# Attention in a diffusion-transformer block: where the softmax's division is applied, on one Trainium2 core

## The chip, the core and the metric

The kernel runs on one core of a Trainium2 chip. The metric is device time in microseconds (us), from launch to end on the core. TensorE (PE in the profile) does the matmuls, with its weight loads in a row of their own (PEld); VectorE (DVE), ScalarE (ACT) and GpSimd (POOL) do elementwise work; SyncE (SP) issues the transfers. TensorE's clock has two levels, 1.2 and 2.4 GHz, and the profile gives the granted clock as a share of the higher one.

## What is computed

One block of a transformer: a feed-forward part, a mixer, a second feed-forward part. The mixer adds a gated scan and a window attention with a sink. What the change touches is the attention: 512 tokens in four blocks of 128, eight heads of width 64 on two key/value heads, each query block against its own key block and the two beside it, and against 256 context keys.

```python
def softmax_with_sink(logits, sink):
    sink_col = jnp.broadcast_to(sink, logits.shape[:-1] + (1,))
    p = jax.nn.softmax(jnp.concatenate([logits, sink_col], axis=-1), axis=-1)
    return p[..., :-1]
...
    p = softmax_with_sink(jnp.concatenate([s_band, s_ctx], axis=-1), sink_b).astype(v.dtype)
    o = (jnp.einsum('bkgnqs,bknsd->bkgnqd', p[..., :3 * BLOCK], vb)
         + jnp.einsum('bkgnqs,bksd->bkgnqd', p[..., 3 * BLOCK:], vc))
```

All tensors are fp32. The kernel multiplies them in a rounded fp32 form (`F32R`) and keeps precision by splitting an operand into a rounded high part and a remainder, each with a matmul of its own.

## The kernel before, in words

`split(hi, lo, src)` (L64 to L66) makes the two parts: a copy with a cast on ACT (L65), a subtraction on DVE (L66). `mm3` (L68 to L74) multiplies split operands in three matmuls: L71, L72 and L74. Nearly all matmuls of the projections stand on these lines.

The instructions are written in program order, but the framework's scheduler puts each engine's instructions in an order of its own, and each engine runs its own list strictly in that order. So an edit in one place can move instructions of other steps on all engines.

The attention works head by head. Head `(g, kv)` is number `kv * 4 + g`; the loop of L1131 to L1141 runs the scores of a head before the output of the head before it.

- `head_scores` (from L1059) makes, for each of the four query blocks `b`, the scores of the band (`sw`) and of the context (`sc`) with four matmuls (L1073, L1075) into two PSUM tiles of the tag `mm`; DVE adds the mask and finds the negated maximum (L1078, L1080); ACT takes the exponential and the sum of it (L1082) into the tile `s`, the probabilities of the block, 512 or 640 columns wide. When all four sums are there, the sink's exponential is added and the reciprocal taken: L1086 on ACT, L1087 and L1088 on DVE, all on 128x4 elements. Then each of the four tiles is scaled by its reciprocal, the first on ACT (L1092), the three others on DVE (L1094).
- `head_out` (from L1097) transposes the probabilities block by block on PE (L1107, with `ident`), splits them (`pth`, `ptl`) and multiplies them with the values: L1113 with the high part, L1114 with the remainder, into one PSUM tile `oo` of the tag `aux`. The value operand holds its own high and low half side by side, so that the two halves of `oo` are added at the end: an ACT copy (L1117) and a DVE sum (L1118) into `ov`, 64x512, which is split into `oah` and `oal`, the input of the merge.

PSUM tiles have two tags, `mm` and `aux`, of four buffers each. `oo` and the transposes take `aux`.

As work to set between the heads' steps, PE has the gate projections (`early_gate`, five of them, 24 matmuls each on L71, L72, L74) and the query projections (`q_pair`, L1041). After the attention come the remaining gates and eight merges (`merge`, L1150), which multiply `oah`/`oal` and the scan's output `rTh`/`rTl` with their output weights.

Beside the merges runs a background task (`mod_gate`, `mod_cols`, in twelve parts by `mod_part`, L635): each part loads eight pieces of `w_ada` into `b7l` (L640), accumulates them on DVE into `b7h` (L643, L645), splits the sum into `mx` and adds over partitions with two matmuls (L654, L655). `b7h` and `b7l` lie in memory that the attention's pool (`ma`) used, so that the first of these loads waits until the attention lets go of it. Nine of the parts run beside the merges, the other matmuls of L654 and L655 later.

```python
            nc.vector.reciprocal(es, es)
            for b in range(NX):
                nw = (min(b + 2, NX) - max(b - 1, 0)) * P
                if b == 0:
                    nc.scalar.activation(probs[b][:, :nw + L], probs[b][:, :nw + L], AF.Copy, scale=es[:, b:b + 1])
                else:
                    nc.vector.tensor_scalar(probs[b][:, :nw + L], probs[b][:, :nw + L], es[:, b:b + 1], None, ALU.mult)
```

Of the kernel before, what the change touches and what calls it, by code (L numbers as in the profile page):

```python
# [16 lines left out]
P = 128  # L17
# [26 lines left out]
def kernel(ctx: ExitStack, tc: tile.TileContext, i, out):  # L44
# [940 lines left out]
    with tc.tile_pool(name="ma", bufs=1, reuse_waits="tile") as ma:  # L985
# [73 lines left out]
        def head_scores(g, kv, qq):  # L1059
# [26 lines left out]
            nc.scalar.activation(es, nms[:, :, 1], AF.Exp, bias=sk[:, h:h + 1])  # L1086
            nc.vector.tensor_tensor(out=es, in0=es, in1=sums, op=ALU.add)  # L1087
            nc.vector.reciprocal(es, es)  # L1088
            for b in range(NX):
                nw = (min(b + 2, NX) - max(b - 1, 0)) * P  # L1090
                if b == 0:
                    nc.scalar.activation(probs[b][:, :nw + L], probs[b][:, :nw + L], AF.Copy, scale=es[:, b:b + 1])  # L1092
                else:
                    nc.vector.tensor_scalar(probs[b][:, :nw + L], probs[b][:, :nw + L], es[:, b:b + 1], None, ALU.mult)  # L1094
            return probs

        def head_out(g, kv, probs):  # L1097
            rr = slice(64 * kv, 64 * kv + 64)
            oo = ps("aux")
            kts = (4, 0, 1, 2, 3, 5)  # L1100
            for u, kt in enumerate(kts):
                bs = range(NX) if kt >= NX else range(max(kt - 1, 0), min(kt + 2, NX))
                pt = ps("aux")
                for b in bs:
                    w0, w1 = max(b - 1, 0), min(b + 2, NX)
                    off = (kt - w0) * P if kt < NX else (w1 - w0 + kt - NX) * P
                    nc.tensor.transpose(pt[:, b * P:(b + 1) * P], probs[b][:, off:off + P], ident)  # L1107
                cc = slice(bs[0] * P, (bs[-1] + 1) * P)
                th = ct([P, T], "pth", F32R, bufs=3, pool=ma)
                tl = ct([P, T], "ptl", F32R, bufs=3, pool=ma)  # L1110
                split(th[:, cc], tl[:, cc], pt[:, cc])
                vk = vs[:, kt, kv].rearrange("p a b -> p (a b)")
                nc.tensor.matmul(oo[:, cc], lhsT=vk, rhs=th[:, cc], start=u == 0, stop=False)  # L1113
                nc.tensor.matmul(oo[:, cc], lhsT=vk, rhs=tl[:, cc], start=False, stop=u == len(kts) - 1)  # L1114

            ov = ct([P, T], "ov", pool=ma)
            nc.scalar.copy(ov[H[0], :], oo[H[1], :])  # L1117
            nc.vector.tensor_tensor(out=ov[rr, :], in0=oo[H[0], :], in1=ov[H[0], :], op=ALU.add)  # L1118
            split(oah[rr, g, :], oal[rr, g, :], ov[rr, :])

        raw_q = []

        def load_q(u):
# [200 lines left out]
```

## Time and profile before

| | us |
|---|---|
| median of 3 runs | 1462.34 (1461.89 to 1462.94) |
| the profiled execution, its own time | 1462.16 |
| its span, first to last instruction | 1460.4 |
| TensorE busy in the span | 1394.3 (95%) |
| VectorE busy | 1144.2 (78%) |
| ScalarE busy | 663.8 (45%) |
| TensorE's mean granted clock | 0.987 |

The sums in the prediction are made against the profiled execution. The attention's score matmuls start at 811.2 us of the span, the last head's sum (L1118) starts at 929.1 us. A matmul's busy time includes its modelled drain, so that neighbours overlap in the record: what a matmul adds in a row of them is read from start to start.

### The profile page before, as it was taken

The numbers are of one execution on the slowest core, as the hardware profiler recorded it, in microseconds if no ns is written. First come the engines' busy times: TensorE is split into PE (matmuls) and PEld (weight loads), VectorE is DVE, ScalarE is ACT, GpSimd is POOL, SyncE is SP. The second block draws the span as 40 slices with busy tenths as digits, with TensorE's granted clock in tenths as the row PEclk, the third lists the DMA queues.
The fourth block names the chain that finished last, engine by engine and source line by source line (L and its number), as shares of the span: only waits on it lengthen the run. The fifth ranks groups of instructions, "written<-read, shape, count | busy, mean of one in ns | idle before, by whom it ended". The sixth has DMA issues, their size and how long they took to land. (4 is left out here: it accounts for less than half of the span.)

```text
span 1460.4 us, 22968 instructions
## 1 busy us (share of the span) xinstructions
PE 1394.3 (95%) x8864; PEld 1233.6 (84%) x8864; DVE 1144.2 (78%) x1995; ACT 663.8 (45%) x1089; POOL 57.6 (4%) x87
## 2 busy tenths in 40 slices
PE   6899999999999998999999899989898999999997
PEld 3699899999999997889898678767677998999996
DVE  6996888888888777485785789777758987787785
ACT  6544333433333346432335689522247543444442
POOL 3200000000000002000001000000010000000001
PEclk9999999999999999999999899999999999999999
DMA  8343343332333232221212111376534543343211
GB/s 299 115 124 97 98 117 99 102 101 87 101 102 93 73 122 68 83 70 34 71 37 85 35 56 30 111 211 197 174 95 140 167 141 101 103 124 101 87 44 58
DMA packets 195765, 151.61 MB, mean 104 GB/s; under 512 B 8392, under 2 KB 186056, under 8 KB 195656
## 3 DMA queue, kind: packets, MB, share of 16 engines
q1 hardware_dynamic: 195656, 150.15, 34.1%
q8 instruction: 69, 1.13, 0.3%
q14 instruction: 40, 0.33, 0.1%
HBM read 148.02 MB, written 2.10 MB: 103 GB/s over the span
## 5 line engine op out<-in xcount | busy, mean ns | idle before, releaser
L66 DVE TENSOR_TENSOR wl<-wraw,wh 128x1024 fp32r<-128x1024 f32 (+1 forms) x180 | 216.8, 1210 | 78.3 <-ACT wh L65 77.1
L65 ACT CAST wh<-wraw 128x1024 fp32r<-128x1024 f32 (+1 forms) x180 | 184.9, 1031 | 143.7 <-PE aux L429 44.0
L71 PE MATMUL mm<-hh,wh 128*128 128x512 f32 (+2 forms) x488 | 172.6, 357 | 0.3 <-ACT gg L972 0.2
L72 PE MATMUL mm<-hl,wh 128*128 128x512 f32 (+2 forms) x488 | 168.7, 354 | 0.4 <-DVE hl L560 0.3
L74 PE MATMUL mm<-hh,wl 128*128 128x512 f32 (+2 forms) x488 | 160.1, 358 | 4.0 <-DVE wl L66 4.0
L428 PE MATMUL mm<-hh,wh 128*128 128x256 f32 (+1 forms) x400 | 122.3, 306 | 3.9 <-DVE sg L506 3.9
L428 PE MATMUL aux<-hh,wh 128*128 128x256 f32 (+1 forms) x400 | 121.8, 304 | 2.0 <-ACT wh L65 2.0
L430 PE MATMUL aux<-hh,wl 128*128 128x256 f32 (+1 forms) x400 | 121.6, 304 | 0.0
L429 PE MATMUL aux<-hl,wh 128*128 128x256 f32 (+1 forms) x400 | 121.5, 304 | 0.0
L430 PE MATMUL mm<-hh,wl 128*128 128x256 f32 (+1 forms) x400 | 121.4, 303 | 0.0
L429 PE MATMUL mm<-hl,wh 128*128 128x256 f32 (+1 forms) x400 | 121.3, 303 | 0.0
L71 PEld LDWEIGHTS mm<-hh,wh 128*128 128x128 f32 x488 | 92.9, 191 | 14.4 <-ACT gg L972 0.7
L72 PEld LDWEIGHTS mm<-hl,wh 128*128 128x128 f32 x488 | 93.2, 191 | 11.4 <-DVE hl L560 1.6
L74 PEld LDWEIGHTS mm<-hh,wl 128*128 128x128 f32 x488 | 88.6, 191 | 12.3 <-DVE wl L66 5.0
L645 DVE SCALAR_TENSOR_TENSOR macc<-wa,cs,macc 128x256 f32<-128x256 f32 x196 | 88.2, 480 | 13.3 <-DMA wa<-w_ada 12.5
L71 PE MATMUL mm<-woh,act 128*128 128x512 f32 x240 | 94.1, 392 | 0.0
L72 PE MATMUL mm<-wol,act 128*128 128x512 f32 x240 | 93.9, 391 | 0.0
L337 DVE TENSOR_TENSOR tok<-tok,mm 128x512 f32<-128x512 f32 x120 | 76.9, 682 | 12.7 <-PE mm L74 12.5
L428 PEld LDWEIGHTS mm<-hh,wh 128*128 128x128 f32 x400 | 75.9, 190 | 6.5 <-DVE sg L506 5.8
L428 PEld LDWEIGHTS aux<-hh,wh 128*128 128x128 f32 x400 | 75.9, 190 | 2.5 <-ACT wh L65 2.5
L429 PEld LDWEIGHTS mm<-hl,wh 128*128 128x128 f32 x400 | 76.0, 190 | 0.6
L430 PEld LDWEIGHTS mm<-hh,wl 128*128 128x128 f32 x400 | 76.0, 190 | 0.0
(389 smaller groups left out, 3451.5 us busy)
## 6 DMA issues: line engine op xcount, KB each, us to landing
wraw<-ffn_w_in SPq DMA_DIRECT2D x88, 512.0 KB, 4.0
wraw<-mix_w_in SPq DMA_DIRECT2D x42, 512.0 KB, 3.7
wa<-w_ada SPq DMA_DIRECT2D x128, 128.0 KB, 2.1
b7l<-w_ada SPq DMA_DIRECT2D x96, 128.0 KB, 2.7
wraw<-ffn_w_out SPq DMA_DIRECT2D x22, 512.0 KB, 3.3
w<-ffn_w_out SPq DMA_DIRECT2D x22, 512.0 KB, 4.5
wa<-w_ada SPq DMA_DIRECT2D x16, 256.0 KB, 4.2
tok<-w_ada SPq DMA_DIRECT2D x16, 256.0 KB, 5.6
```

The source lines that it names most:

```text
L65: nc.scalar.copy(hi, src)
L66: nc.vector.tensor_tensor(out=lo, in0=src, in1=f32(hi), op=ALU.subtract)
L71: nc.tensor.matmul(o, lhsT=sh, rhs=mh, start=start, stop=False)
L72: nc.tensor.matmul(o, lhsT=sh, rhs=ml, start=False, stop=False)
L74: nc.tensor.matmul(o, lhsT=sl, rhs=mh, start=False, stop=stop)
L337: nc.vector.tensor_tensor(out=y, in0=y, in1=o[h], op=ALU.add)
L428: nc.tensor.matmul(o, lhsT=wk, rhs=mh, start=first and k == 0, stop=False, skip_group_check=True)
L429: nc.tensor.matmul(o, lhsT=wk, rhs=ml, start=False, stop=False, skip_group_check=True)
L430: nc.tensor.matmul(o, lhsT=wl[:, k0 + k, :], rhs=mh, start=False, stop=k == H4 - 1, skip_group_check=True)
L645: nc.vector.scalar_tensor_tensor(out=a, in0=w, scalar=cs[:, v, k:k + 1], in1=a, op0=ALU.mult, op1=ALU.add)
```

## The change

The probabilities stay unscaled. The reciprocals, 128 queries by four blocks, are split into a high part and a remainder (`eh`). In `head_out` eight matmuls per head, two for each query block, spread them over partitions: the stationary operand is one column of `eh` repeated 128 times, the moving operand is the identity in the rounded form (`identr`, made once), so that the PSUM tile `pe` holds, in each of its rows, the reciprocal of query `t` in column `t`. Once the head's output `ov` is summed, one more DVE operation multiplies it with `pe`. In the changed program the lines from L1089 on have other numbers: the transposes are L1104, the value matmuls L1110 and L1111, the spreading matmuls L1117, the sum L1121, the new product L1122.

```diff
             nc.vector.reciprocal(es, es)
-            for b in range(NX):
-                nw = (min(b + 2, NX) - max(b - 1, 0)) * P
-                if b == 0:
-                    nc.scalar.activation(probs[b][:, :nw + L], probs[b][:, :nw + L], AF.Copy, scale=es[:, b:b + 1])
-                else:
-                    nc.vector.tensor_scalar(probs[b][:, :nw + L], probs[b][:, :nw + L], es[:, b:b + 1], None, ALU.mult)
-            return probs
-
-        def head_out(g, kv, probs):
+            eh = [ct([P, NX], f"eh{n}", F32R, bufs=2, pool=ma) for n in range(2)]
+            split(eh[0], eh[1], es)
+            return probs, eh
+
+        def head_out(g, kv, probs_eh):
+            probs, eh = probs_eh
...
+            pe = ps("aux")
+            for b in range(NX):
+                for n in range(2):
+                    nc.tensor.matmul(pe[:, b * P:(b + 1) * P], lhsT=view(eh[n], b, [(0, P)]), rhs=identr,
+                                     start=n == 0, stop=n == 1)
             ov = ct([P, T], "ov", pool=ma)
             nc.scalar.copy(ov[H[0], :], oo[H[1], :])
             nc.vector.tensor_tensor(out=ov[rr, :], in0=oo[H[0], :], in1=ov[H[0], :], op=ALU.add)
+            nc.vector.tensor_tensor(out=ov[rr, :], in0=ov[rr, :], in1=pe[rr, :], op=ALU.mult)
             split(oah[rr, g, :], oal[rr, g, :], ov[rr, :])
 
+        identr = ct([P, P], "identr", F32R, pool=ma)
+        nc.scalar.copy(identr, ident)
```

The scheduler's order moves with it. In these lists a row is line, operation, output, inputs (for a matmul the moving operand, then the stationary one) and shape, "x2" a repetition.

On VectorE, during the second head's scores, the list before has the first head's three scalings (tiles `s_7934` to `s_7954`) between two steps of the second head:

```order
L1078 ISA s_7994,nms_7966<-mm_7988,lr_7653,nsk_7657 128x384
L1078 ISA nms_7966 128x1
L1094 TENSOR_SCALAR s_7934<-s_7934,es_7958 128x640
L1094 TENSOR_SCALAR s_7944<-s_7944,es_7958 128x640
L1094 TENSOR_SCALAR s_7954<-s_7954,es_7958 128x512
L1080 TENSOR_SCALAR s_7994,nms_7966<-mm_7989,nms_7966 128x256
L1078 ISA s_8004,nms_7966<-mm_7998,lr_7653,nsk_7657 128x256
```

Now the remainder of the reciprocals (`eh_1289`) stands at that place, with the second head's steps around it and the first head's remainders (`ptl`) after them:

```order
L1078 ISA s_7996,nms_7968<-mm_7990,lr_7653,nsk_7657 128x384
L1078 ISA nms_7968 128x1
L66 TENSOR_TENSOR eh_1289_7965<-es_7960,eh_1288_7964 128x4
L1078 ISA s_8006,nms_7968<-mm_8000,lr_7653,nsk_7657 128x256
L1078 ISA nms_7968 128x1
L1080 TENSOR_SCALAR s_7996,nms_7968<-mm_7991,nms_7968 128x256
L1080 TENSOR_SCALAR s_8006,nms_7968<-mm_8001,nms_7968 128x256
L66 TENSOR_TENSOR ptl_8025<-aux_8019,pth_8024 128x512
```

The three scalings left that place, and one small operation came. The new product, L1122, stands between the head's sum (L1121) and the remainder of its split.

On TensorE, before, the second head's scores end and the first gate projection (L71, L72, L74) begins with the first head's first transposes (L1107) between its matmuls:

```order
L1073 MATMUL mm_7999<-kk_7660,qq_1261_7864 128x256
L1075 MATMUL mm_7999<-kl_1235_7662,qq_1261_7864 128x256
L71 MATMUL mm_7915<-hh_5031,wh_8085 128x512
L72 MATMUL mm_7915<-hl_5032,wh_8085 128x512
L1107 MATMUL aux_8017<-ident_61,s_7924 128x128
L1107 MATMUL aux_8017<-ident_61,s_7934 128x128
L74 MATMUL mm_7915<-hh_5031,wl_8086 128x512
```

Now transposes (L1104) and the first value matmul (L1110) of the first head stand between the second head's scores, ahead of that gate:

```order
L1073 MATMUL mm_8000<-kk_7660,qq_1262_7866 128x256
L1075 MATMUL mm_8000<-kl_1235_7662,qq_1262_7866 128x256
L1110 MATMUL aux_8018<-pth_8024,vs_7742 128x512
L1104 MATMUL aux_8030<-ident_61,s_7926 128x128
L1073 MATMUL mm_8001<-kk_7660,qq_1262_7866 128x256
L1075 MATMUL mm_8001<-kl_1235_7662,qq_1262_7866 128x256
L1104 MATMUL aux_8030<-ident_61,s_7936 128x128
L1104 MATMUL aux_8039<-ident_61,s_7926 128x128
L1104 MATMUL aux_8039<-ident_61,s_7936 128x128
L1104 MATMUL aux_8039<-ident_61,s_7946 128x128
L71 MATMUL mm_7917<-hh_5031,wh_8097 128x512
```

Nine transposes and one value matmul of the first head moved ahead of the first gate matmul; there were none before.

At the last head's end, TensorE's list before has gate matmuls between the last value matmuls:

```order
L71 MATMUL mm_9151<-hh_5031,wh_9147 128x512
L1114 MATMUL aux_9024<-ptl_9060,vs_7742 128x384
L1113 MATMUL aux_9024<-pth_9068,vs_7742 128x256
L72 MATMUL mm_9151<-hl_5032,wh_9147 128x512
L1114 MATMUL aux_9024<-ptl_9069,vs_7742 128x256
L1113 MATMUL aux_9024<-pth_9079,vs_7742 128x512
L74 MATMUL mm_9151<-hh_5031,wl_9148 128x512
```

Now the last head's spreading matmuls (`identr`) are there:

```order
L1110 MATMUL aux_9096<-pth_9140,vs_7742 128x256
L1104 MATMUL aux_9146<-ident_61,s_9008 128x128
L1117 MATMUL aux_9157<-identr_7819,eh_1565_9016 128x128
L1111 MATMUL aux_9096<-ptl_9141,vs_7742 128x256
L1117 MATMUL aux_9157<-identr_7819,eh_1566_9017 128x128
L1117 MATMUL aux_9157<-identr_7819,eh_1565_9016 128x128
L1110 MATMUL aux_9096<-pth_9151,vs_7742 128x512
```

Between the first score matmul and the attention's last one, 208 matmuls of L71, L72 and L74 stood before and 188 stand now; of the 20 that moved, 7 come between the attention's end and the ninth part of the background task, 13 behind it. On the engines' lists nothing is changed ahead of the attention.

## Rows read from the trace of the kernel before

**Rows 1.** The page: busy time of the engines, and the span in 40 slices.

```profile
PE 1394.3 (95%) x8864; PEld 1233.6 (84%) x8864; DVE 1144.2 (78%) x1995; ACT 663.8 (45%) x1089; POOL 57.6 (4%) x87
PE   6899999999999998999999899989898999999997
DVE  6996888888888777485785789777758987787785
PEclk9999999999999999999999899999999999999999
```

**Rows 2.** Windows: stretch, length, busy PE, PEld, DVE, ACT, POOL, clock, DMA share, GB/s.

```profile
810.00:823.00 13.00, 7.86 (x31) 5.88 (x30) 12.10 (x35) 8.95 (x17) 1.27 (x1) 0.73 0.14 40
823.00:840.00 17.00, 17.00 (x82) 13.76 (x82) 10.45 (x29) 11.46 (x24) 0.00 (x0) 0.90 0.14 41
840.00:932.00 92.00, 88.77 (x485) 71.77 (x484) 78.00 (x202) 77.44 (x147) 2.57 (x2) 1.00 0.13 39
932.00:1036.00 104.00, 95.85 (x415) 75.28 (x414) 81.38 (x160) 30.40 (x45) 0.00 (x0) 1.00 0.68 202
```

**Rows 3.** Waits of PE, 840 to 932 us: who, for whom, us, times, longest.

```profile
PE aux L1113 <- ACT pth L65: 0.8, 1, 0.8
PE mm L1073 <- DVE nms L1078: 0.7, 2, 0.6
PE aux L1114 <- DVE ptl L66: 0.5, 2, 0.4
PE mm L1073 <- DVE s L1080: 0.5, 1, 0.5
PE mm L71 <- ACT gg L972: 0.2, 1, 0.2
```

**Rows 4.** Waits of PE, 932 to 1050 us.

```profile
PE aux L654 <- ACT mx L65: 7.5, 6, 2.1
PE mm L72 <- DVE wol L66: 3.8, 1, 3.8
```

**Rows 5.** Groups of DVE, 823 to 930 us: the removed scaling, and its neighbours in kind.

```profile
L1094 DVE TENSOR_SCALAR s<-s,es 128x640 f32<-128x640 f32 (+1 forms) x24 | 11.2, 526 | 0.1
L1118 DVE TENSOR_TENSOR ov<-aux,ov 64x512 f32<-64x512 f32 x8 | 5.5, 682 | 2.4 <-ACT ov L1117 2.3
L1087 DVE TENSOR_TENSOR es<-es,sums 128x4 f32<-128x4 f32 x7 | 1.1, 163 | 3.3 <-ACT es L1086 3.2
```

**Rows 6.** Single lines on ACT: duration in ns, min/median/max, first and last start.

```profile
L1092 ACT ACTIVATE s<-s,es x8: 709/729/737, 823.3 to 916.7; 128x512 f32<-128x512 f32 x8
L1086 ACT ACTIVATE es<-nms,sk x8: 281/282/285, 822.0 to 914.7; 128x4 f32<-128x4 f32 x8
L1117 ACT COPY ov<-aux x8: 582/584/587, 835.3 to 928.5; 64x512 f32<-64x512 f32 x8
```

**Rows 7.** Timeline of ACT, then the DMA queue of SP (SPq), at two places.

```profile
823.31 0.71 ACT L1092 ACTIVATE s<-s,es 128x512 f32<-128x512 f32 x1
826.81 0.59 ACT L65 CAST pth<-aux 128x512 fp32r<-128x512 f32 x1 [1.98 <-PE aux L1107]
...
932.19 2.00 SPq L640 DMA_DIRECT2D b7l<-w_ada  x4
```

**Rows 8.** Timeline of PE in three places: start us, us, instruction, count.

```profile
643.48 2.50 PE L887 MATMUL aux<-vt,KT 128*128 128x128 f32 x20
645.81 0.39 PE L905 MATMUL aux<-vt,A 128*128 128x128 f32 x2
...
777.47 1.47 PE L962 MATMUL aux<-ident,gs 128*128 128x128 f32 x12
778.70 0.48 PE L71 MATMUL mm<-hh,wh 128*128 128x512 f32 x1
...
834.91 0.40 PE L71 MATMUL mm<-hh,wh 128*128 128x512 f32 x1
...
836.07 0.39 PE L74 MATMUL mm<-hh,wl 128*128 128x512 f32 x1
```

**Rows 9.** A group of PE by line and shape, whole span: the scan's matmuls.

```profile
L887 PE MATMUL aux<-vt,KT 128*128 128x128 f32 x80 | 10.0, 280 | 0.1
```

## The prediction

> **What bounds the kernel now.** I read the page's busy line first, to see which engine could set the time at all. TensorE is busy for 95% of the span, VectorE for 78%, and the slices show PE near full almost everywhere [rows 1]. An average does not say what the attention waits for, so I then cut the stage with the windows view. The reader is to see three different stretches [rows 2]. From 810 to 823 us VectorE is busy 12.10 of 13.00 us and PE only 7.86: the first scores wait for VectorE, and the clock granted is 0.73 there, a mix of its two levels. From 823 to 932 us PE is busy 105.77 of 109 us while VectorE has 88.45: PE leads, with VectorE and ScalarE (77.44 of 92) not far behind. From 932 to 1036 us, beside the merges, PE stands for 8.15 us of 104.
>
> Third I read the waits of PE itself, since a busy neighbour costs nothing if PE does not stop for it. Between 840 and 932 us they come to 2.7 us in all [rows 3]: 0.8 us for a cast of transposed probabilities, the rest for score steps, remainders and a gate's copy. None names a scaling (L1092, L1094). After 932 us PE stops 7.5 us for the background task's casts and once 3.8 us for output weights [rows 4].
>
> So the reading is: in the stage that the change touches, PE's list is the bound from 823 us on, and the change takes work from VectorE and ScalarE and gives work to PE.
>
> **The change part by part.**
>
> *The scalings that go.* 24 on VectorE take 11.2 us [rows 5], 8 on ScalarE 8 x 0.729 = 5.8 us [rows 6]. This lies beside a PE that hardly waits for it, so its removal is worth on the path only what it takes from PE's waits.
>
> *What VectorE and ScalarE get.* The product with `pe` is priced by the sum ahead of it, same shape, one operand in PSUM: 8 x 0.682 = 5.5 us [rows 5]. The remainder of 128x4 costs what the addition of 128x4 costs, 8 x 0.163 = 1.3 us [rows 5]. The cast of 128x4 on ScalarE goes by the activation of that shape, 8 x 0.282 = 2.3 us [rows 6]; `identr` is one cast more, under 0.6 us by the 128x512 cast [rows 7], once. VectorE is relieved of 11.2 - 5.5 - 1.3 = 4.4 us net, ScalarE of 5.8 - 2.3 - 0.6 = 2.9 us. The product stands in the chain of a head's end, 0.68 us between the sum and the split of `ov`. Behind the waiting product on VectorE is the split's remainder and then the next head's steps; the merge reads the result only after the list's gate matmuls, so I cost this delay at nothing except for the last head, where it would be 0.7 us if that cover were missing.
>
> *The matmuls that come.* Eight per head, 64 in all, 128 columns wide, each with a weight load of its own. No row shows a 128-column matmul in the rounded form. The nearest by shape is the scan's: 20 records from 643.48 to 645.81 us, 0.1165 us each [rows 8]. The transposes, also 128 columns with a load each, are below it: 12 from 777.47 to 778.70 us, 0.1025 us [rows 8]. From above: a full fp32 matmul of that width takes two records (the 40 of L887 leave 80 [rows 9]), so 0.233 us if the rounded form does not help at this width. I take 0.1165, as it is an ordinary matmul and not a transpose: 64 x 0.1165 = **+7.5 us**; bounds 6.6 and 14.9 us.
>
> The Trainium skill, in TensorE: Matmul & The Clock Gate, section Back-to-back issue gap, gives about 81 ns per matmul for a stream of load and matmul pairs at 128 columns. By it the 64 would cost 5.2 us, and with the other terms below the time would be about 1463.7 us. The rows here are slower, and no row shows this form at this width; the sum goes by the rows.
>
> *What moves, first head.* Nine transposes and one value matmul now stand between the second head's scores, where PE is idle for 13.00 - 7.86 = 5.1 us [rows 2]. They can, because they no longer wait for the reciprocal and the scalings: before, the first head's scaling on ScalarE starts at 823.31 and its first transposed cast at 826.81 us [rows 7]. They leave the full stretch after it: 9 x 0.1025 + 0.23 = **-1.2 us**. From below nothing, if VectorE, still the bound there, does not let the scores through between them.
>
> *PE's waits from 840 to 932 us.* With VectorE and ScalarE lighter some of the 2.7 us [rows 3] go. None stands right behind a scaling, so from below it is nothing, from above 2.7. I take a third, **-0.9 us**.
>
> *What moves, after the attention.* 20 gate or merge matmuls leave the attention's list. Five steps of that kind take from 834.91 to 836.07 us, so 0.23 us each [rows 8]: 4.6 us. The first `w_ada` load waits for the attention's memory at 932.19 us [rows 7] and starts the background task, which PE then waits for [rows 4]. The 7 that now come before the task's ninth part fall where PE waits for it, **-1.6 us**; the other 13 come behind it and stay paid. SP's list has these loads one weight load sooner; with DMA at 0.68 of its time there [rows 2] I count nothing for it, since the task's start hangs on the attention's end.
>
> *Sum.* 7.5 - 1.2 - 0.9 - 1.6 = +3.8 us. Against the profiled execution, 1462.16 us (span 1460.4, 1.8 us around it), that is 1466.0 us. The median of the runs shown, 1462.34, lies 0.2 us above this execution, so I leave it there. A measurement of this kernel can tell about 0.2%, 2.9 us, from no change; the sum is just outside.
>
> **The rivals.**
>
> *VectorE paces the attention (faster).* The mechanism: from 840 to 932 us VectorE and ScalarE are busy 78.00 and 77.44 of 92 us [rows 2], and PE's small waits could be only the tail of a list ordered around them. Then the stage shortens by VectorE's relief, 4.4 us, and PE fits the new matmuls into room that busy time, with its overlapping drains, does not show: 1457.8 us. It decides from the point where PE, after the change, still waits for VectorE as often as in rows 3. Against it: 2.7 us of waits are less than the 4.4 us to be gained. Chance 0.20.
>
> *The matmuls are absorbed (no change).* PE stands 8.15 us from 932 to 1036 us, 7.5 of it for the background task [rows 2, 4]. If the moved work falls there wholly, not for 7 of 20 matmuls alone, 4.6 instead of 1.6 us are hidden, and with half of the other waits of rows 3 the sum is 7.5 - 1.2 - 1.4 - 4.6 = +0.3: 1462.5 us. For it: the task's nine parts pace that stage. Against it: 13 of the 20 stand behind the ninth part. Chance 0.29.
>
> *The matmuls are dear (slower still).* At 0.233 us each the sum is 14.9 - 3.7 = +11.2: 1473.4 us. The same end has another road, on which the change does not loosen the head's chain but tightens it: `pe` holds one of four `aux` buffers from the spreading until the product, 0.58 + 0.68 + 0.68 = about 1.9 us with the copy [rows 6], the sum and the product [rows 5], and the next head's transposes wait for it. At half the heads this is 4 x 1.9 = 7.6 us on top of the sum, 1473.6 us. Against it: the order puts the spreading at a head's end, when its own transposes are done. Chance 0.08.
>
> **How the numbers follow.** The forecast, PE pays for most of the new matmuls, has 0.43; its own range is 1465 to 1468.5, from the lower bound of the matmuls with all of the 3.7 us regained to their price with nothing regained but the first head's 1.2. Slower by over 0.2% is 0.43 + 0.08 = 0.51, within it 0.29, faster 0.20. The range over all cases is 1459.5 to 1472: the low end leaves out the larger part of the VectorE case (some 0.12), the high end the larger part of the dear one (some 0.06).
>
> **What would show it.** Right: the 64 matmuls stand start to start at 0.10 to 0.12 us; VectorE's busy time between 823 us and the attention's end falls by 4 to 5 us and PE's rises; the first `w_ada` load of the background task starts later than 932.19 us by 1 to 2 us, although 20 matmuls left the stretch; the waits of PE for the task's casts shrink from 7.5 us. Wrong: that load starts earlier than 932 us (then VectorE paced the stage), or the waits of PE in the attention grow with the name of an `aux` tile (then PSUM is short), or the stage after the attention changes by more than 3 us by its new order alone, which no row of mine bounds.

## The result, and the profile after

The change makes the kernel slower: 1471.13 us (1470.87 to 1471.33, three runs) against 1462.34, a ratio of 1.0062 with a 95% interval of 1.0047 to 1.0077. That is 8.8 us, where the prediction said 3.8 and a range up to 1472. The profiled execution's span went from 1460.4 to 1469.5 us.

The page of the changed kernel, busy time of the engines, to be read against [rows 1]:

```profile
PE 1402.8 (95%) x8928; PEld 1240.3 (84%) x8928; DVE 1142.4 (78%) x1987; ACT 660.2 (45%) x1090; POOL 58.3 (4%) x87
```

PE has its 64 instructions more and 8.5 us more of busy time; VectorE only 1.8 us less over the whole span. The windows view of the four stretches of [rows 2], same columns:

```profile
810.00:823.00 13.00, 8.28 (x35) 6.14 (x34) 11.90 (x33) 8.76 (x17) 1.28 (x1) 0.74 0.14 40
823.00:840.00 17.00, 16.66 (x88) 13.86 (x87) 9.13 (x26) 10.90 (x24) 0.00 (x0) 1.00 0.14 42
840.00:932.00 92.00, 86.42 (x486) 69.80 (x485) 70.87 (x190) 70.75 (x141) 3.36 (x2) 1.00 0.15 45
932.00:1036.00 104.00, 96.42 (x420) 75.19 (x419) 80.98 (x154) 32.16 (x46) 0.00 (x0) 1.00 0.62 185
```

From 840 to 932 us VectorE is busy 70.87 instead of 78.00 us and ScalarE 70.75 instead of 77.44, but PE falls too, from 88.77 to 86.42: all three stand more. The attention ends later (its last value matmul began at 928.05 us before; its last three spreading matmuls now begin from 935.14 us on). The waits of PE, from 840 us to that end, then after it:

```profile
PE aux L1110 <- ACT pth L65: 3.2, 7, 0.7
PE mm L1073 <- DVE s L1080: 0.8, 2, 0.5
PE aux L1111 <- DVE ptl L66: 0.5, 2, 0.3
PE mm L1073 <- DVE nms L1078: 0.3, 1, 0.3
PE aux L1104 <- DVE ov L1122: 0.2, 1, 0.2
```

```profile
PE aux L654 <- ACT mx L65: 7.7, 10, 1.5
PE mm L71 <- ACT oah L65: 0.4, 1, 0.4
```

Against [rows 3] the wait of the value matmuls for the cast of transposed probabilities went from 0.8 us, once, to 3.2 us, seven times; the named waits (those that the waits view lists) sum to 5.0 instead of 2.7 us. Only the last line, 0.2 us, is a wait for `pe`'s release. Against [rows 4] the wait of 3.8 us for output weights is gone.

The timeline of PE in the changed kernel shows where such a wait falls: transposes, a run of spreading matmuls, and then a value matmul whose cast is not there.

```profile
911.14 0.27 PE L1104 MATMUL aux<-ident,s 128*128 128x128 f32 x1
911.25 0.38 PE L1111 MATMUL aux<-ptl,vs 128*128 128x256 f32 x1
911.47 1.00 PE L1117 MATMUL aux<-identr,eh 128*128 128x128 f32 x8
913.21 0.51 PE L1110 MATMUL aux<-pth,vs 128*128 128x512 f32 x1 [0.73 <-ACT pth L65]
```

The groups of VectorE from 823 to 937 us answer to [rows 5]: the product costs what the sum costs.

```profile
L1121 DVE TENSOR_TENSOR ov<-aux,ov 64x512 f32<-64x512 f32 x8 | 5.5, 684 | 6.5 <-ACT ov L1120 6.5
L1122 DVE TENSOR_TENSOR ov<-ov,aux 64x512 f32<-64x512 f32 x7 | 4.8, 684 | 0.5
```

The timelines of ScalarE and of SP's queue answer to [rows 7]: the first head's first cast comes 3.9 us earlier, and the first four `w_ada` loads come from 919.48 us on, not from 932.19.

```profile
822.96 0.59 ACT L65 CAST pth<-aux 128x512 fp32r<-128x512 f32 x1 [0.46 <-PE aux L1104]
```

```profile
919.48 1.77 SPq L640 DMA_DIRECT2D b7l<-w_ada  x4
```

**The granted clock moved too.** Before, TensorE's clock was at its lower level (0.50) from 816 to 826 us, while PE stood much of the time beside the first scores, and again from 1041 to 1048 us, in and after a wait of PE of 3.8 us for output weights (1039.9 to 1043.7 us). In the changed kernel it is back at 1.00 by 823 us, and beside the merges, where that wait is gone, it does not fall. Windows of before (first two lines) and of the changed kernel (third), columns as in [rows 2], and PE's timeline before:

```profile
823.00:826.00 3.00, 3.00 (x12) 2.51 (x12) 2.88 (x13) 1.83 (x5) 0.00 (x0) 0.50 0.00 0
1041.00:1048.00 7.00, 4.27 (x10) 3.40 (x11) 6.13 (x10) 0.82 (x1) 0.00 (x0) 0.53 0.51 134
823.00:826.00 3.00, 2.80 (x18) 2.31 (x17) 2.46 (x13) 3.00 (x9) 0.00 (x0) 1.00 0.00 0
```

```profile
1043.73 1.22 PE L72 MATMUL mm<-wol,mgh 128*128 128x512 f32 x2 [3.80 <-DVE wol L66]
1044.75 1.05 PE L74 MATMUL mm<-woh,mgl 128*128 128x512 f32 x2
1045.60 1.05 PE L72 MATMUL mm<-wol,mgh 128*128 128x512 f32 x2
```

At the lower level two matmuls of 512 columns take 0.85 us from start to start, 0.43 us each, and 0.23 at the higher. PE is "busy" there and still loses time, so neither the busy share nor a wait shows it.

**Where the 9.1 us of the span came from.** I cut each profiled execution at three starts on PE, read from its timeline, where a row of several matmuls counts by its first: the first score matmul, the attention's last value or spreading matmul (in spread_last the last of a row of eight), and the last row of the output projection that follows the merges. "Filler" is the number of gate and merge matmuls that the list has inside the attention. "Idle" is my estimate of what PE stands in the attention: its length less the list's matmuls at their start-to-start times (0.2275, 0.175 and 0.117 us for 512, 384 and 256 columns, 0.1025 for a transpose, 0.11 for a spreading matmul); it holds what matmuls lose at the lower clock, too. The kernels of the experiments are in the same table; "against before" is the ratio times 1462.3, with an interval of some 2 to 3 us to each side, while the stages are those of one execution (that of no_division is 3.8 us below the median of its runs, that of before_kts 2.4 above).

| kernel | against before | up to attention | attention | filler | idle in it | merges, output projection | rest |
|---|---|---|---|---|---|---|---|
| before | | 811.2 | 116.8 | 208 | 21.5 | 164.5 | 367.9 |
| changed | +9.1 | 811.4 | 123.7 | 188 | 25.8 | 164.2 | 370.2 |
| no_division | -5.4 | 809.3 | 112.0 | 198 | 19.0 | 161.6 | 369.9 |
| product_alone | -7.3 | 810.1 | 111.7 | 201 | 18.0 | 160.8 | 370.9 |
| both | +5.7 | 810.4 | 126.1 | 198 | 25.9 | 161.4 | 367.9 |
| held | -3.1 | 812.4 | 115.9 | 199 | 20.8 | 160.4 | 370.3 |
| high_alone | +3.5 | 812.0 | 120.3 | 203 | 22.6 | 164.3 | 370.4 |
| doubled | +12.0 | 809.6 | 129.2 | 182 | 25.6 | 164.2 | 369.9 |
| mm_tag | +8.6 | 810.0 | 123.5 | 174 | 28.8 | 168.5 | 369.4 |
| matmuls_alone | +9.4 | 809.3 | 125.4 | 189 | 27.3 | 165.4 | 369.6 |
| spread_last | +8.3 | 813.0 | 122.6 | 201 | 21.7 | 163.1 | 371.5 |
| dma_spread | +1.3 | 810.1 | 116.8 | 201 | 23.1 | 167.2 | 368.9 |
| dma_rows | -7.2 | 811.7 | 113.0 | 201 | 19.3 | 160.8 | 370.5 |
| before_kts | 0.0 | 810.7 | 117.0 | 208 | 21.7 | 165.4 | 371.3 |

The work ahead of the attention is the same in all, and its length scatters from 809.3 to 813.0 us: in a single execution a stage's length means something from 2 us up.

So 6.9 us of the change lie in the attention: 2.6 of work (7.0 for the spreading matmuls, less 20 fillers) and 4.3 of standing. The stage after it is 0.3 us shorter although it took over those 20 matmuls: the wait for output weights and the stretch at the lower clock are gone from it. The rest, 2.3 us longer, cannot be put down to the change: the control `before_kts`, which does the work of before in kind and number, has 3.4 us there. In both, the granted clock is 0.96 from 1130 to 1170 us, where before has 1.00.

The clock can be compared over all runs as well. Its mean is 0.9876 in the runs of before that stand beside the first experiments, 0.9898 in no_division, 0.9905 in product_alone and 0.9907 in the changed kernel. One minus the clock, times the span, is the full-speed time that was not granted: 18.2, 14.9, 13.8 and 13.7 us. So, as an estimate from above, up to 3.3 us of what no_division gains and up to 4.4 us of what product_alone gains can be the clock's; between product_alone and the changed kernel the clock makes no difference.

### The profile page after: what moved, and what is told of

Same layout as the page of the kernel before. It is cut to its first block, busy times and chain, and to the rows that moved or that the text cites. A ratio compares the mean times of both kernels' runs of the same rounds, so it can differ in the third digit from the quotient of the medians.

```text
span 1469.5 us, 23087 instructions
## 1 busy us (share of the span) xinstructions
PE 1402.8 (95%) x8928; PEld 1240.3 (84%) x8928; DVE 1142.4 (78%) x1987; ACT 660.2 (45%) x1090; POOL 58.3 (4%) x87
## 5 line engine op out<-in xcount | busy, mean ns | idle before, releaser
L71 PE MATMUL mm<-hh,wh 128*128 128x512 f32 (+2 forms) x488 | 171.2, 355 | 0.1
L72 PE MATMUL mm<-hl,wh 128*128 128x512 f32 (+2 forms) x488 | 167.9, 353 | 0.2
L74 PE MATMUL mm<-hh,wl 128*128 128x512 f32 (+2 forms) x488 | 159.2, 356 | 4.2 <-DVE wl L66 4.2
L71 PEld LDWEIGHTS mm<-hh,wh 128*128 128x128 f32 x488 | 92.6, 191 | 14.3 <-DVE hh L559 0.3
L72 PEld LDWEIGHTS mm<-hl,wh 128*128 128x128 f32 x488 | 92.8, 190 | 11.4 <-DVE hl L560 1.0
L74 PEld LDWEIGHTS mm<-hh,wl 128*128 128x128 f32 x488 | 88.3, 190 | 12.5 <-DVE wl L66 5.2
L645 DVE SCALAR_TENSOR_TENSOR macc<-wa,cs,macc 128x256 f32<-128x256 f32 x196 | 88.3, 481 | 12.5 <-DMA wa<-w_ada 12.0
L71 PE MATMUL mm<-woh,act 128*128 128x512 f32 x240 | 94.1, 392 | 0.2 <-ACT sg L511 0.2
L72 PE MATMUL mm<-wol,act 128*128 128x512 f32 x240 | 93.8, 391 | 0.0
L337 DVE TENSOR_TENSOR tok<-tok,mm 128x512 f32<-128x512 f32 x120 | 76.9, 682 | 12.5 <-PE mm L74 12.4
```

Source lines behind the costliest of these rows:

```text
L71: nc.tensor.matmul(o, lhsT=sh, rhs=mh, start=start, stop=False)
L72: nc.tensor.matmul(o, lhsT=sh, rhs=ml, start=False, stop=False)
L74: nc.tensor.matmul(o, lhsT=sl, rhs=mh, start=False, stop=stop)
L337: nc.vector.tensor_tensor(out=y, in0=y, in1=o[h], op=ALU.add)
L645: nc.vector.scalar_tensor_tensor(out=a, in0=w, scalar=cs[:, v, k:k + 1], in1=a, op0=ALU.mult, op1=ALU.add)
```

## The experiments

Three theories stood at the start. A: PE's list pays for the 64 matmuls, and the scalings were free. B: the head's end, the PSUM buffer that `pe` holds or the longer chain, costs several us beyond them. C: the order that the scheduler makes of the lists moves the time by 2 us or more, whatever is edited.

**Without the division.**

```diff
-            eh = [...]; split(eh[0], eh[1], es)
...
-            pe = ps("aux")
-            ... the spreading matmuls
...
-            nc.vector.tensor_tensor(out=ov[rr, :], in0=ov[rr, :], in1=pe[rr, :], op=ALU.mult)
```

> The changed kernel without the division altogether: no scaling, no spreading matmuls, no pe, no product (the output's heads stay unscaled). Theory A, PE's list pays for the 64 spreading matmuls and the scalings were free: before and this kernel differ only by what left PE's waits, so 1460.5 to 1462.5 us. Theory B, the longer end of a head (pe in a buffer of aux, the product in the chain) costs several us beyond the matmuls: the same number here, since both are gone. Theory C, the time follows the order that the scheduler makes of the lists and where loads then land, so that stages which the edit does not touch move by 2 us or more: anything from 1459 to 1465. If VectorE paced the attention, 1458 or less.

Measured: ratio 0.9963 (0.9949 to 0.9976), 5.4 us faster than before. The scalings were not free: their removal is worth more than all that PE was named to wait for in [rows 3], though up to 3.3 us of it can be the clock's. The attention is 4.8 us shorter with 10 fillers (2.3 us) fewer, and the stage after it gains 2.9 us until the output projection's end.

**Scalings and spreading together.**

```diff
             eh = [ct([P, NX], f"eh{n}", F32R, bufs=2, pool=ma) for n in range(2)]
             split(eh[0], eh[1], es)
+            for b in range(NX):
+                ... the scalings of before
```

> The scalings of before and the spreading matmuls with the product, in one kernel (the heads come out scaled twice). It has the whole cost of the change without its relief. Theory A: before plus 64 matmuls at 0.10 us, 1469 to 1471 us, so that against the changed kernel nothing or at most 2 us is lost by the scalings' return. Theory B: 1471 to 1474, since the head's end is as long as in the changed kernel and VectorE has 11 us more to do. Theory C: no order by cost among these kernels, from 1467 to 1475.

Measured: 1.0039 (1.0025 to 1.0053), +5.7 us, with the changed kernel's idle in the attention (25.9 and 25.8 us). On top of the scalings the spreading costs, over the whole kernel, about its price, but not because it is cheap in the attention: that is 9.3 us longer than before with 10 fillers fewer, and 3.1 us come back behind it, where PE waits 0.4 instead of 3.8 us for output weights and the granted clock stays at 1.00. Beside the spreading the scalings cost nothing; this kernel's ratio is rather below the changed one's. The relief that the first run showed is there only without the spreading.

**The product without the spreading.**

```diff
-            pe = ps("aux")
-            ... the spreading matmuls
...
+        onet = ct([P, T], "onet", pool=ma)
+        nc.vector.memset(onet, 1.0)
...
-            nc.vector.tensor_tensor(out=ov[rr, :], in0=ov[rr, :], in1=pe[rr, :], op=ALU.mult)
+            nc.vector.tensor_tensor(out=ov[rr, :], in0=ov[rr, :], in1=onet[rr, :], op=ALU.mult)
```

> The changed kernel with the product kept but with a tile of ones in SBUF as its second operand: no spreading matmuls and no pe in PSUM (the output's heads stay unscaled). Theory A: the changed kernel less 64 matmuls at 0.10 us, 1464 to 1465 us. Theory B: if the PSUM buffer is what costs, all 8.8 us and the relief go too, 1460.5 to 1462.5; if the product's place in the chain is what costs, 1465 to 1467. Theory C: a difference of over 2 us outside the attention.

Measured: 0.9950 (0.9934 to 0.9967), -7.3 us, faster than any theory had it. Eight products in the chain of a head's end cost nothing that can be seen, as the prediction said. From here to the changed kernel it is 16.4 us, for 64 matmuls and their PSUM tile; the clock has no part in that (0.9905 and 0.9907). PE's waits from 840 to 922 us in this kernel, in full, have none for a cast of probabilities:

```profile
PE mm L1073 <- DVE s L1080: 0.9, 2, 0.5
PE aux L1104 <- DVE ov L1116: 0.5, 2, 0.3
```

**Half of the matmuls.**

```diff
-                for n in range(2):
-                    nc.tensor.matmul(..., start=n == 0, stop=n == 1)
+                for n in range(1):
+                    nc.tensor.matmul(..., start=n == 0, stop=n == 0)
```

> The changed kernel with one spreading matmul for each query block, with the high part alone: 32 instead of 64 (the reciprocal is then rounded). Theory A: half of the matmuls' price goes, 3.3 us, so 1467 to 1468.5 us. Theory B: what costs is held once per head, so it stays: 1470 to 1471. Theory C: 1465 to 1471 with the difference in other stages than the attention.

Measured: 1.0024 (1.0012 to 1.0037), +3.5 us, 10.8 above the product alone. The attention takes 8.6 us more than there. Half of the matmuls, at their price 3.4 us, bring over half of the loss.

After these four runs the question was what makes 64 matmuls cost 16 us: A2 says that each is dear by itself, B that the held buffer is, D that price and hold add up.

**One wide matmul per head, the buffer held as long.**

```diff
-            for b in range(NX):
-                for n in range(2):
-                    nc.tensor.matmul(pe[:, b * P:(b + 1) * P], ...)
+            nc.tensor.matmul(pe, lhsT=view(eh[0], 0, [(0, P)]), rhs=view(identr, 0, [(0, NX), (1, P)]),
+                             start=True, stop=True)
```

> The changed kernel with one spreading matmul per head instead of eight: 512 columns, block 0's reciprocal for all four blocks (so three blocks are scaled by the wrong reciprocal). pe, its buffer of aux and the product stay as they are; 8 matmuls instead of 64. From the first four runs, against before: the product alone -7.3 us, 32 matmuls +3.5, 64 matmuls +9.1, so the 64 with their pe cost some 16 us, where their pitch in a run, 0.11 us, makes 7. Theory A2, each small matmul costs some 0.25 us wherever it stands (a weight load that is not covered): 8 more than the product alone at 0.25 us, so before less 5 us. Theory B, the buffer that pe holds costs 6 to 9 us whatever is computed into it: before plus 1 to 4 us. Theory C (order and landings): neither, by 2 us or more to a side.

Measured: 0.9979 (0.9966 to 0.9991), -3.1 us, 4.2 above the product alone, of which eight matmuls of 512 columns are 1.8. From the first spreading matmul to the product's end `pe` is held for 4.9 us per head on average here, 4.6 in the changed kernel, so the hold is the same. What the buffer costs by being held is the remaining 2.4 us at most, with an uncertainty of that size. Theory B as the main cost falls.

**`pe` from the other PSUM tag.**

```diff
-            pe = ps("aux")
+            pe = ps()
```

> The changed kernel with pe taken from the four mm buffers (scores, gates) instead of the four aux buffers; same 64 matmuls. Theory A2: as the changed kernel, before plus 8 to 10 us. Theory B: if aux is what was short, PE's waits for the cast of transposed probabilities return from 3.2 to under 1 us and the time falls to before plus 0 to 4 us; if the mm buffers are then short instead, the waits turn up at the score matmuls and the time stays. Theory C: before plus 3 to 12 us, with 34 gate matmuls fewer in the attention than before had.

Measured: 1.0059 (1.0041 to 1.0077), +8.6 us, as the changed kernel, although `pe` is held for 10.7 us per head here. The waits for the casts did not go; from 840 us to the attention's end they are the largest two:

```profile
PE aux L1111 <- DVE ptl L66: 3.5, 4, 1.6
PE aux L1110 <- ACT pth L65: 2.5, 3, 1.6
```

**All spreading matmuls twice.**

```diff
-                for n in range(2):
-                    nc.tensor.matmul(..., lhsT=view(eh[n], ...), ..., stop=n == 1)
+                for n in range(4):
+                    nc.tensor.matmul(..., lhsT=view(eh[n % 2], ...), ..., stop=n == 3)
```

> The changed kernel with all spreading matmuls issued twice, 128 instead of 64, into the same pe (so the output's heads come out doubled). Theory A2: 64 more at 0.25 us, 16 us above the changed kernel, before plus 24 to 26 us. Theory B: the buffer is held once, the second 64 cost their pitch of 0.11 us, 7 us, before plus 15 to 17 us. Theory C: between, or under 15.

Measured: 1.0082 (1.0062 to 1.0102), +12.0 us, 2.9 above the changed kernel. That a small matmul costs 0.25 us wherever it stands (theory A2) is out: 64 more would be 16. The changed kernel's own trace says the same: 47 times something other than a value matmul follows a spreading matmul, and each time it starts within 0.14 us. The idle is 25.6 us, as with 64. So the standing comes with the first 64 and did not grow with more in this execution.

**The matmuls, with nobody reading `pe`.**

```diff
-            nc.vector.tensor_tensor(out=ov[rr, :], in0=ov[rr, :], in1=pe[rr, :], op=ALU.mult)
+            nc.vector.tensor_tensor(out=ov[rr, :], in0=ov[rr, :], in1=onet[rr, :], op=ALU.mult)
...
+        onet = ct([P, T], "onet", pool=ma)
+        nc.vector.memset(onet, 1.0)
```

> The changed kernel with its 64 spreading matmuls into pe, but nobody reads pe: the product reads a tile of ones in SBUF (the output's heads stay unscaled). The buffer of aux comes free as soon as the eight matmuls end, not after the copy, the sum and the product. Against before, so far: product alone -7.3 us, held (8 matmuls) -3.1, 32 matmuls +3.5, 64 +9.1, 128 +12.0. Theory D, the matmuls at their pitch of 0.11 us (7 us) and the hold until the product (some 3 to 8 us) add up: without the hold before plus 0 to 3 us. Theory A2, a small matmul among others is dear by itself: before plus 7 to 10 us. Theory C, the order alone scatters by 3 us: between the two.

Measured: 1.0064 (1.0051 to 1.0077), +9.4 us, as the changed kernel. Neither the product's reading of PSUM nor the hold until the product makes the loss; theory D falls with it. PE's waits from 840 to 935 us:

```profile
PE mm L1073 <- DVE nms L1078: 2.2, 3, 1.6
PE aux L1110 <- ACT pth L65: 1.9, 5, 0.7
PE mm L1073 <- DVE s L1080: 0.8, 2, 0.5
PE aux L1111 <- DVE ptl L66: 0.5, 2, 0.3
```

**The spreading pinned behind the head's last value matmul.** By now PE's standing was the suspect, and its place in the changed list: a run of spreading matmuls ahead of a value matmul, where gate matmuls had covered the cast (theory E). `last` is the head's last matmul of L1111.

```diff
-                nc.tensor.matmul(oo[:, cc], lhsT=vk, rhs=tl[:, cc], ...)
+                last = nc.tensor.matmul(oo[:, cc], lhsT=vk, rhs=tl[:, cc], ...)
...
+            with tc.issue_after(last.ins):
                 for b in range(NX):
                     ...
```

> The changed kernel with one thing pinned: the spreading matmuls of a head are issued behind the head's last value matmul (an edge of issue order, no wait). The work is the changed kernel's. In its list the eight stand in one run behind L1111, none between transposes and value matmuls, and 201 gate and merge matmuls are in the attention's stretch, as in the product alone (188 in the changed kernel). Theory E: the 64 cost their pitch, 0.11 us, and the rest of the 16 us is that they took the places ahead of value matmuls where gate matmuls of 0.23 us had covered the casts, so that PE waits for pth and ptl; pinned, PE's waits for pth fall from 3.4 us to under 1, and the time is the product alone plus 7: before less 2 to before plus 2 us. Theory A2, a small matmul costs 0.25 us wherever it stands: before plus 8 to 10 us, as the changed kernel. Theory B, pe's buffer: the hold now ends just as late and starts later, before plus 4 to 8 us.

Measured: 1.0057 (1.0036 to 1.0078), +8.3 us. Theory E falls as an account of the whole loss. It holds for the wait it named: the 13 fillers are back in the attention, the waits for `pth` are 1.4 us, the idle is 21.7 instead of 25.8 us. But the attention is only some 1 us shorter, and 10.9 us longer than with the product alone at the same 201 fillers: 7.0 for the matmuls, nearly 4 for standing, now mostly at the score matmuls. The time itself says less: the seven runs scatter from 1464.29 us (clock 0.993) to 1474.86 (0.987), and at their mean clock of 0.988 up to 4 us more is not granted than in the changed kernel. Part of what E gains may be hidden there. PE's waits from 840 to 935 us, the main ones:

```profile
PE mm L1073 <- DVE nms L1078: 2.3, 3, 0.9
PE mm L1073 <- DVE s L1080: 1.7, 2, 1.2
PE aux L1110 <- ACT pth L65: 1.4, 3, 0.6
```

Its runs of eight give the price most clearly. The timeline of PE at the first head's end:

```profile
832.21 0.42 PE L1111 MATMUL aux<-ptl,vs 128*128 128x512 f32 x1
832.46 1.00 PE L1118 MATMUL aux<-identr,eh 128*128 128x128 f32 x8
833.30 0.44 PE L72 MATMUL mm<-hl,wh 128*128 128x512 f32 x1
```

The next matmul starts 0.84 us after the first of the eight, 0.84 or 0.85 at all eight heads: 0.105 us each, 6.7 us for 64.

**A control for theory C.**

```diff
-            kts = (4, 0, 1, 2, 3, 5)
+            kts = (5, 0, 1, 2, 3, 4)
```

> A control: the kernel before with the two context blocks swapped in the order in which a head's output takes its key blocks (5 first and 4 last, not 4 first and 5 last). The work is the same, instruction for instruction in kind and number. Theory D: no change, within 1.5 us of before. Theory C, the place of instructions in the lists is worth some us by itself: 2 us or more to either side.

Measured: 1.0000 (0.9990 to 1.0011). An order changed in this small way is worth nothing that can be told. A swap that leaves the list's shape as it is says little of one that moves 20 matmuls, so C is narrowed, not out. What the control does show is the stage after the output projection: 371.3 us against 367.9, with 2.6 instead of 1.0 us in the longest wait for `sg`. The first line is before's, from 1090 us on, the second the control's:

```profile
PE mm L428 <- DVE sg L506: 2.9, 5, 1.0
```

```profile
PE mm L428 <- DVE sg L506: 4.8, 5, 2.6
```

**The spreading by transfers.** What the matmuls do, a broadcast over partitions, the queues can do without PE and without PSUM (`dr` is a pool in DRAM, `sa` the tile `scr`).

```diff
-            eh = [...]; split(eh[0], eh[1], es)
+            scr = dr.tile([NX, P], F32, tag="scr", name=nm("scr"), bufs=2)
+            nc.sync.dma_start(scr.rearrange("b t -> t b"), es)
+            eh = ct([P, T], "pe", bufs=2, pool=ma)
+            ...
+            nc.sync.dma_start(eh[64 * kv:64 * kv + 64, :], AP(sa.tensor, sa.offset, [[0, 64], [1, T]]))
...
-            pe = ps("aux")
-            ... the spreading matmuls
...
-            nc.vector.tensor_tensor(out=ov[rr, :], in0=ov[rr, :], in1=pe[rr, :], op=ALU.mult)
+            nc.vector.tensor_tensor(out=ov[rr, :], in0=ov[rr, :], in1=eh[rr, :], op=ALU.mult)
```

> The changed kernel with the reciprocals spread by two transfers per head (to a scratch row in DRAM and back to 64 partitions) in place of the matmuls: no PE work, no PSUM, the product reads SBUF. Same result as the changed kernel. Theories A2 and B: both costs are gone, so it comes out near the product alone, before less 4 to 8 us, if the transfers land before a head's sum, some 10 us after the reciprocals. Theory C, or the transfers being late or holding up the weight loads behind them on SP's queue: before less 2 us to before plus 6 us, with PE waiting for wh or wl or for an aux tile.

Measured: 1.0009 (0.9998 to 1.0020). The matmuls' loss is gone, but VectorE waits for the spread tile. Its waits from 823 to 930 us (first line; 9.1 us with the last head's, up to 945 us), and the timeline of SP's queue:

```profile
DVE ov L1121 <- DMA pe<-scr: 5.1, 1, 5.1
```

```profile
822.00 0.37 SPq L1091 DMA_DIRECT2D scr<-es  x1
830.95 0.52 SPq L1094 DMA_DIRECT2D pe<-scr  x1
```

The read starts 9 us after the write of 512 pieces of 4 bytes; at the other heads it is 9 to 12. The Trainium skill, DMA: Bandwidth & Descriptors, section Rules for kernel authors, says that a strided last dimension is lowered to one descriptor per element, and to rearrange it so that the last dimension is contiguous; the trace fits that (528 packets pass from 820 to 832 us, 144 from 820 to 826 us in the next run, each window with the first write and little else), and the next run follows the advice.

**The same in whole rows.**

```diff
-            scr = dr.tile([NX, P], F32, tag="scr", name=nm("scr"), bufs=2)
-            nc.sync.dma_start(scr.rearrange("b t -> t b"), es)
+            scr = dr.tile([P, NX], F32, tag="scr", name=nm("scr"), bufs=2)
+            nc.sync.dma_start(scr, es)
...
-            nc.vector.tensor_tensor(out=ov[rr, :], in0=ov[rr, :], in1=eh[rr, :], op=ALU.mult)
+            nc.vector.tensor_tensor(out=ov[rr, :], in0=ov[rr, :], in1=view(eh[rr, :], 0, [(1, NX), (NX, P)]), op=ALU.mult)
```

> The spread by transfers again, with the tile of reciprocals written to the scratch as it lies (128 rows of 16 bytes), read back as one row for 64 partitions, and the product reading it with a stride of four. In the run before this one the write in the other order, 512 pieces of 4 bytes, stood 9 to 12 us ahead of the read, and VectorE waited 9.1 us for pe. Theory D: the write now takes some 2 us, VectorE no longer waits for pe, and the kernel comes out near the product alone: before less 4 to 7 us. If the strided product costs over 0.68 us or the waits on SP's queue hold up weight loads, before less 3 us to no change; if the write takes as long as before, before plus 1 us.

Measured: 0.9951 (0.9938 to 0.9963), -7.2 us: it computes what the changed kernel computes and is faster than both kernels, against before by the same 7 us as the product alone. As there, up to 4.9 us of this can be the clock's (0.9904 on average, against 0.9871 in the runs of before beside it). The write of 128 rows of 16 bytes is followed by the read after 1.4 us at four heads and 2.2 to 3.3 us at the others, in the timeline of SP's queue at the first head:

```profile
823.67 0.34 SPq L1091 DMA_DIRECT2D scr<-es  x1
825.12 0.52 SPq L1094 DMA_DIRECT2D pe<-scr  x1
```

The product's stride has a price, 1.080 instead of 0.684 us (groups of VectorE, 823 to 930 us), and VectorE has room for it:

```profile
L1121 DVE TENSOR_TENSOR ov<-ov,pe 64x512 f32<-64x512 f32 x8 | 8.6, 1080 | 0.2
```

## Why the prediction was right in sign and short in size

- *The price of the matmuls* was right: 6.7 to 7.0 us against +7.5. The pitch is 0.105 us, near the transposes' end of the bounds. The 81 ns per load and matmul that the Trainium skill gives (TensorE: Matmul & The Clock Gate, Back-to-back issue gap) is not what these runs show. The dear form (0.233 us each) is out.
- *What VectorE gets* was right: 0.684 and 0.158 us for product and remainder, and VectorE's busy time in the attention fell by 5.0 us. *The product's delay at nothing* was right.
- *The first head's move, -1.2*, came out in size by luck. The gaps between PE's starts, beyond the pitches, fell by 1.3 us up to 840 us. But 1.0 of it lies between 823 and 826.5 us, where the granted clock was 0.50 before and is 1.00 now; the mechanism forecast, matmuls that fill PE's idle time up to 823 us, brought four more of them there (35 against 31), not ten. [rows 2] had shown a clock of 0.90 from 823 to 840 us, and the prediction took PE as fully used there.
- *PE's waits, -0.9, is the step that failed.* The prediction took it that lighter neighbours could only shorten PE's 2.7 us of waits [rows 3]. As a bound on the relief alone that was not far off from 840 us on: with the spreading left out, the gaps beyond the pitches fall from 11.4 to 9.3 us there (product_alone), by 2.1. What it did not see is that PE stands longer once the spreading is on its list: 17.1 us, 5.7 more than before, where -0.9 stood. Of the 7.8 us of idle between product_alone (18.0) and the changed kernel (25.8) none is the matmuls' own time. About 6 us of it stand ahead of value matmuls (gaps of 8.8 us in all, 2.7 in product_alone) and 2 ahead of score matmuls (12.5 and 10.5).
- *What the relief is worth in the whole kernel*, 5 to 7 us (no_division, product_alone, dma_rows), is more than the prediction's terms could give, but not through waits in the attention alone: in product_alone's execution that stage's gaps shrink by some 3.5 us, the lower clock up to 826 us included, and the stage after it gives 3.7 us, although it took over 7 fillers. There the wait for output weights is 2.0 instead of 3.8 us and the clock stays at 1.00. Which of the two brings how much is not shown.
- *The moved matmuls after the attention, -1.6 of 4.6* was too small: that stage took all 20 and is 0.3 us shorter. The matmuls were not hidden behind the background task, as forecast (PE's waits for its casts went from 7.5 to 7.7 us instead of shrinking). Room came from the wait for `wol`, 3.8 us before and gone now, and from the stretch of some 7 us at the lower clock that went with it; where a list's order puts such a weight is not in any of my rows.
- *SP's list at nothing*: the first `w_ada` load came 12.7 us earlier, not 1 to 2 us later. By the prediction's own sign this would have meant that VectorE paced the stage. It was a bad sign: the attention did end later, and only these four loads came sooner. Nor does the trace show that the attention's memory held them back: before, they stood on SP's list behind a weight load (L96), which waited 18.1 us for VectorE (`wl`) and was issued at 931.77 us; now they stand ahead of that load, which is issued at 943.07.
- *Of the rivals*, VectorE's pacing was the nearest to what product_alone and dma_rows show, 1457.8 us predicted, 1455 to 1457 by the ratios of dma_rows, product_alone and no_division, but only for a change that adds nothing to PE, and its mechanism is not shown by that: PE's gaps from 840 us on fell by 2.1 us, not by 4.4. The second road of the dear rival, the `aux` buffer, is not it, although `pe` is held for 4.6 us per head, not 1.9: 0.2 us of named wait, at most some 2 us by `held`, nothing regained in mm_tag and matmuls_alone. The sign set for it, waits under the name of an `aux` tile, did grow (0.8 to 3.2 us), but these are waits for a cast and not for a buffer.

In sum, the change gives back the relief and pays for the matmuls: -7.3 us by the product alone, +6.7 for the matmuls, and 9.7 more. Of those 9.7 the table accounts for 7.8 as standing of PE inside the attention; nearly 4 of it are left when the spreading is pinned, though the time is then no better by more than the runs' scatter. What stays open is why PE stands longer as soon as eight small matmuls per head are on its list: the order that follows from them, or a coupling of PE, ScalarE and VectorE that this account by lists does not hold. The waits change their names with each variant (casts, remainders, scores), and no run here held the rest of the list fixed.

## What to carry to other kernels

The waits of a full engine in one stage do not say what relief of its neighbours brings to the kernel: here about 2 of 5 to 7 us came out of that stage's full part, the rest out of its start and the stage behind it, where other weights were late and the granted clock was low. So take the work out alone and measure it before trading it, and compare the granted clock of every stage before a cause is named. What a small matmul costs is its pitch only if the list around it stays as it is; here somewhat more than its price again was lost in standing. A broadcast over partitions can go through the transfer queues where they idle and there is time for it; whole rows took 1.4 to 3.3 us here, single elements 9 to 12.

## What the runs showed of the hardware that was not expected

- A matmul in the rounded form, 128 columns, weights with a stride of zero: 0.105 us start to start in runs of eight, with its own load each (load records of 0.187 to 0.192 us overlap).
- A write of 128x4 reciprocals to DRAM: 9 to 12 us until the next transfer on it starts with 512 pieces of 4 bytes, 1.4 to 3.3 us with 128 rows of 16 bytes.
- VectorE reading one SBUF operand with a stride of 16 bytes: 1.080 us for 64x512 (dma_rows), against 0.684 without a stride, in SBUF (dma_spread) as in PSUM (the changed kernel). The Trainium skill, SBUF — State Buffer, section Door 1: The DMA port swizzle, speaks of 16-byte lines of which at least two hits are needed for full speed; with one element per line the trace agrees that it is slower.
- The granted clock of before fell to 0.50 from 1041 to 1048 us, in and after a wait of PE of 3.8 us beside the merges; matmuls of 512 columns took 0.43 instead of 0.23 us each. The changed kernel, without that wait, kept 1.00 beside the merges.
